# DoRA forward pass on one core: the first two stores issued two chunks earlier, and three small loads held back until the first store has landed

## The chip, the cores and the metric

One core of one Trainium2 chip. The metric is the device time of one execution in microseconds (us).

## The reference

```python
# x [16, 2048, 256], W [256, 256], lora_A [256, 16], lora_B [16, 256], m [256], scale = 1.0
W_adapted = W + scale * (lora_A @ lora_B)
W_norm = np.sqrt(np.sum(W_adapted ** 2, axis=0, keepdims=True) + 1e-8)
W_final = W_adapted / W_norm * m
y = x.reshape(-1, 256) @ W_final          # 32768 rows in, 32768 rows out
```

33.6 MB of x come in, 33.6 MB of y go out, and the weights are small.

## The kernel before

The 32768 rows are 8 blocks of 4096 rows, each of 8 chunks of 512 rows (64 chunks, 0-63). There is room on chip for five blocks. A block is loaded into a buffer, its chunks go through GpSimd (cast to bf16), TensorE (transpose and product), VectorE and ScalarE, and ScalarE copies each result chunk back over the x that it came from. The buffer is then stored and, once stored, loaded again with a later block. So blocks 5, 6 and 7 wait for the stores of blocks 0, 1 and 2.

All loads are issued by the sync engine on one queue, in order, all stores by the scalar engine on another. The number after a chunk range is the chunk behind whose copy the store is issued:

```python
loads = [(0, 2), (2, 2), (4, CH - 4)] + units[1 : XBUFS - 1]
loads += [((XBUFS - 1) * CH, CH - 3)]                          # block 4, chunks 32-36: 20 KB packets
loads += [(XBUFS * CH - 3 + c, 1) for c in range(3)] + units[XBUFS:]   # 37, 38, 39: 4 KB packets each
# ... (cut)
F = NBLK - XBUFS                                               # 3
G = F * CH                                                     # 24
stores = [(b * CH, CH, 21 + b) for b in range(F - 1)]          # blocks 0 and 1: 32 KB packets
stores += [(G - CH, CH // 2, 24), (G - CH // 2, CH // 2, 24)]  # block 2, two halves: 16 KB packets
FIRST = len(stores)
stores += [(G + c, 1, G + 3) for c in range(4)]                # chunks 24-27, 4 KB packets each
stores += [(G + 4, CH - 4, 47)]
stores += [(b * CH, CH, max(47, (b + 1) * CH - 1)) for b in range(F + 1, NBLK - 1)]
stores += [(g0, cnt, g0 + cnt - 1) for g0, cnt in units[-2:]]
HALF = FIRST - 2
# ... (cut)
for n in range(len(loads)):
    if loads[n][0] == XBUFS * CH:                              # block 5 waits for the first three stores
        for k in range(HALF + 1):
            nc.sync.wait_ge(sem(f"store{k}"), 16)
    if loads[n] == units[-1]:
        nc.sync.wait_ge(sem(f"store{HALF + 1}"), 16)
    load_x(n)
# ... (cut) GpSimd, one pair of chunks at a time:
    if p == REST:                                              # REST = 15
        nc.gpsimd.wait_ge(sem(f"store{HALF}"), 16)             # rests until the third store has landed
```

Each transfer is split over 16 DMA engines, 8 data packets per engine, one packet per partition. A packet of 32 KB takes 1.213 us, of 20 KB 0.766, of 16 KB 0.611, of 4 KB 0.159 (medians of this trace). These figures come from the trace's list of DMA packets, which gives the start, duration, size and queue of each but not its engine; I call them the packet records below. A time "per engine" is a sum over all packets divided by 16.

Of the kernel before, what the change touches and what calls it, by code (L numbers as in the profile page):

```python
# [11 lines left out]
def kernel(  # L12
# [10 lines left out]
    nc = tc.nc  # L23
# [19 lines left out]
    XBUFS = 5  # L43
    CH = DJ // J
# [59 lines left out]
    loads = [(0, 2), (2, 2), (4, CH - 4)] + units[1 : XBUFS - 1]  # L104
# [8 lines left out]

    F = NBLK - XBUFS
    G = F * CH
    stores = [(b * CH, CH, 21 + b) for b in range(F - 1)]
    stores += [(G - CH, CH // 2, 24), (G - CH // 2, CH // 2, 24)]
    FIRST = len(stores)
    stores += [(G + c, 1, G + 3) for c in range(4)]
# [9 lines left out]
    def sem(name):  # L129
        if name not in sems:  # L130
            sems[name] = tc.alloc_semaphore(name)
        return sems[name]
# [10 lines left out]
    def load_x(n):  # L143
        nc.sync.dma_start(
            out=in_sbuf(*loads[n]), in_=in_dram(x_flat, *loads[n])
        ).then_inc(sem(f"load{n}"), 16)
# [13 lines left out]
    nc.scalar.dma_start(out=b_nat[:], in_=lora_B).then_inc(sem("load_b"), 16)  # L160
    nc.scalar.dma_start(out=m_row[:], in_=m[None, :]).then_inc(sem("load_m"), 16)
    for n in range(len(loads)):
        if loads[n][0] == XBUFS * CH:


# [5 lines that stand above are left out]
# [13 lines left out]
    for p in range(NPR):  # L184
        b, c = divmod(p, PRB)
# [66 lines left out]
    for g in range(NCH):  # L252
        b, c = divmod(g, CH)
# [123 lines left out]
```

## Time and profile before

| | |
|---|---|
| median, 6 runs beside the changed kernel | 162.49 us (162.26 to 162.74) |
| span of the profiled run | 161.3 us |
| packet time, both queues, per engine | 158.4 us |
| empty DMA time before 4 us; from 158 us to the last packet's end at 160.8 (packet records) | 2.3 us; 1.0 us |
| last store issued | 132.2 us |

The page, its slices, the windows and the chain are shown in the prediction below. In short: the DMA engines are full from 3.2 us to the end, and no compute engine is. The first is from the table of waits, the others from GpSimd's timeline (start, duration, what, and in brackets the idle time before it and what ended it):

```profile
POOL xb L197 <- DMA out_dram<-x_sb: 27.7, 1, 27.7
```

```profile
93.86 5.57 POOL L197 CAST xb<-x_sb 128x2048 bf16<-128x2048 f32 x3 [3.25 <-DMA x_sb<-in_x_dram]
99.65 1.89 POOL L197 CAST xb<-x_sb 128x2048 bf16<-128x2048 f32 x1 [0.22 <-PE xt_ps L302]
```

GpSimd rests 27.7 us for the third store. Later it waits 3.25 us for the load of block 5.

### The profile page before, as it was taken

The page shows a single profiled execution, that of the slowest core. Times are in us where ns is not written, and L with a number is a line of the kernel's source. Part 1 is how long each engine was busy: PE and PEld are TensorE (multiplying, and loading weights), DVE is VectorE, ACT ScalarE, POOL GpSimd, SP SyncE. Part 2 cuts the span into 40 slices and gives each one's busy share as a digit, 9 for nine tenths or more (in the row PEclk, how much of TensorE's full clock was granted, in tenths as well). Part 3 has the DMA queues.
Part 4 walks back from the last instruction along what each step waited for, and adds up shares of the span by engine and source line. Part 5 has one row for each costly group of instructions (what it writes and reads, how often), then busy time and mean ns, then how long its engine had stood idle before and what let it go on. Part 6 is the DMA issues. An engine that isn't in the chain of part 4 may idle for free. (4 is left out here: it accounts for less than half of the span.)

```text
span 161.3 us, 2012 instructions
## 1 busy us (share of the span) xinstructions
PE 95.2 (59%) x786; PEld 83.8 (52%) x786; DVE 46.6 (29%) x44; ACT 63.9 (40%) x67; POOL 62.9 (39%) x39
## 2 busy tenths in 40 slices
PE   0491899999999700000199999999999940000000
PEld 0160799999998600000179989989899930000000
DVE  0439635353635300000033535353445300000000
ACT  3010076868686520000027675856776850000000
POOL 1085339776764000000674479198676200000000
PEclk9999999999999995555559999999999998555555
DMA  4999999999899999989999999999999999999995
GB/s 163 427 455 459 390 504 406 390 488 423 374 412 361 511 423 390 473 374 451 427 482 414 386 463 421 407 433 433 422 484 419 406 479 414 400 479 423 386 443 228
DMA packets 4356, 67.42 MB, mean 418 GB/s; under 512 B 625, under 2 KB 642, under 8 KB 1666
## 3 DMA queue, kind: packets, MB, share of 16 engines
q1 hardware_dynamic: 2160, 33.82, 49.5%
q10 hardware_dynamic: 2194, 33.59, 48.7%
q14 instruction: 2, 0.02, 0.0%
HBM read 33.85 MB, written 33.55 MB: 418 GB/s over the span
## 5 line engine op out<-in xcount | busy, mean ns | idle before, releaser
L256 ACT COPY x_sb<-y_ps 128x1024 f32<-128x1024 f32 x64 | 62.0, 1014 | 60.0 <-PE y_ps L316 57.8
L197 POOL CAST xb<-x_sb 128x2048 bf16<-128x2048 f32 x32 | 60.4, 1900 | 61.3 <-DMA out_dram<-x_sb 27.7
L316 PE MATMUL y_ps<-w_final,xt 128*128 128x256 bf16 x512 | 63.6, 278 | 1.2 <-PEq L291 1.1
L238 DVE COPY xt<-xt_ps 128x1024 f32<-128x1024 f32 x32 | 39.2, 1224 | 72.6 <-PE xt_ps L302 72.6
L316 PEld LDWEIGHTS y_ps<-w_final,xt 128*128 128x128 bf16 x512 | 51.1, 100 | 8.5 <-issue 1.9
L302 PE MATMUL xt_ps<-identity,xb 128*128 128x128 f32 x264 | 37.0, 287 | 28.2 <-PEq L291 28.2
L302 PEld LDWEIGHTS xt_ps<-identity,xb 128*128 128x128 f32 x264 | 31.7, 148 | 30.3 <-issue 30.0
L283 PE MATMUL y_ps<-sq,ones 128*128 128x256 f32 x4 | 2.1, 674 | 1.6 <-DVE sq L223 1.6
L272 PE MATMUL y_ps<-identity,a_nat 128*16 128x128 f32 x2 | 0.6, 394 | 4.1 <-DMA a_nat<-in_lora_A_dram 4.1
L248 ACT ACTIVATE norm<-y_ps,eps_col 128x256 f32<-128x256 f32 x1 | 0.5, 473 | 5.8 <-PE y_ps L283 5.8
L234 DVE TENSOR_TENSOR w_final<-wam,rnorm 128x256 bf16<-128x256 f32 x2 | 2.5, 1266 | 0.0
L283 PEld LDWEIGHTS y_ps<-sq,ones 128*128 128x128 f32 x4 | 1.2, 326 | 2.3 <-DVE sq L223 2.1
L272 PEld LDWEIGHTS y_ps<-identity,a_nat 128*16 128x16 f32 x2 | 0.1, 88 | 4.1 <-issue 4.1
L246 ACT ACT_TABLE_LOAD x1 | 1.3, 1283 | 2.4 <-issue 2.4
L203 POOL MEMSET xb<- 128x2048 bf16 x1 | 1.8, 1804 | 0.7 <-PE xt_ps L302 0.7
L231 DVE RECIPROCAL rnorm<-norm 128x256 f32<-128x256 f32 x1 | 1.7, 1747 | 0.0
L225 DVE COPY m_all<-y_ps 128x256 f32<-128x256 f32 x1 | 0.4, 424 | 3.3 <-PE y_ps L288 3.3
L214 DVE CAST b_bf<-b_nat 16x256 bf16<-16x256 f32 x1 | 0.3, 281 | 3.5 <-DMA b_nat<-in_lora_B_dram 3.5
L288 PE MATMUL y_ps<-m_row,ones 1*128 1x256 f32 x2 | 1.2, 706 | 0.0
L276 PE MATMUL y_ps<-b_bf,aT 16*128 16x256 bf16 x2 | 0.6, 404 | 0.7 <-DVE aT L216 0.7
L219 DVE SCALAR_TENSOR_TENSOR wa<-y_ps,w_nat 128x512 f32<-128x512 f32 x1 | 0.7, 692 | 0.8 <-PE y_ps L276 0.8
L288 PEld LDWEIGHTS y_ps<-m_row,ones 1*128 1x128 f32 x2 | 0.5, 308 | 0.6 <-issue 0.6
(13 smaller groups left out, 3.3 us busy)
## 6 DMA issues: line engine op xcount, KB each, us to landing
x_sb<-in_x_dram SPq DMA_DIRECT2D x5, 4096.0 KB, 26.5
out_dram<-x_sb ACTq DMA_DIRECT2D x5, 4096.0 KB, 22.7
out_dram<-x_sb ACTq DMA_DIRECT2D x5, 2048.0 KB, 29.0
x_sb<-in_x_dram SPq DMA_DIRECT2D x3, 2048.0 KB, 31.4
x_sb<-in_x_dram SPq DMA_DIRECT2D x1, 2560.0 KB, 44.8
x_sb<-in_x_dram SPq DMA_DIRECT2D x2, 1024.0 KB, 6.1
out_dram<-x_sb ACTq DMA_DIRECT2D x4, 512.0 KB, 50.1
x_sb<-in_x_dram SPq DMA_DIRECT2D x3, 512.0 KB, 46.4
```

The lines of the kernel that those rows point to most:

```text
L197: nc.gpsimd.tensor_copy(out=xb_bufs[p % NXB][:], in_=x_bufs[b % XBUFS][:, 2 * c * J : 2 * (c + 1) * J, :],).then_inc(sem("rounded"), 1)
L203: nc.gpsimd.memset(xb_bufs[NPR % NXB][:], 0.0).then_inc(sem("rounded"), 1)
L219: nc.vector.scalar_tensor_tensor(out=wa[:], in0=ab_ps, scalar=float(scale), in1=w_nat[:], op0=ALU.mult, op1=ALU.add).then_inc(dv, 1)
L231: nc.vector.reciprocal(out=rnorm[:], in_=norm[:]).then_inc(dv, 1)
L234: i = nc.vector.tensor_mul(out=w_final[:, t], in0=wam[:, t], in1=rnorm[:])
L238: nc.vector.tensor_copy(out=xt_bufs[p % NXT][:].rearrange("p r t -> p (r t)").bitcast(FP32), in_=xt_ps[p % 2][:],).then_inc(sem("copied"), 1)
L246: nc.scalar.activation(out=warm[:], in_=eps_col[:], func=AF.Sqrt)
L256: nc.scalar.copy(out=x_bufs[b % XBUFS][:, c * J : (c + 1) * J, :], in_=y_ps[g % 2][:]).then_inc(sem("room"), 1)
L283: i = nc.tensor.matmul(n2_ps, ones[:], sq[:, t, :], start=(t == 0), stop=(t == KC - 1))
L288: nc.tensor.matmul(mb_ps, ones[0:1, :], m_row[:], start=True, stop=True).then_inc(pe, 1)
L302: i = nc.tensor.transpose(xt_ps[p % 2][:, j * P : (j + 1) * P], xb_bufs[p % NXB][:, j, :].bitcast(FP32), identity[:],)
L316: i = nc.tensor.matmul(y_ps[h][:, j, :], xt_bufs[p % NXT][:, r : r + P, t], w_final[:, t, :], start=(t == 0 and (j % (J // 2)) == 0), stop ...
```

## The change

Intent: to have the first result on its way out earlier, and to keep the small loads out of its way until it has landed.

```diff
-    stores = [(b * CH, CH, 21 + b) for b in range(F - 1)]
+    stores = [(b * CH, CH, 19 + b) for b in range(F - 1)]
 ...
     for n in range(len(loads)):
+        if loads[n][0] == XBUFS * CH - 3:
+            nc.sync.wait_ge(sem("store0"), 16)
         if loads[n][0] == XBUFS * CH:
```

## The prediction

> **What bounds the kernel now.** I first read the head of the page and its slices, because a kernel that moves 67 MB in 161 us may be bound by moving it.
>
> ```profile
> span 161.3 us, 2012 instructions
> PE 95.2 (59%) x786; PEld 83.8 (52%) x786; DVE 46.6 (29%) x44; ACT 63.9 (40%) x67; POOL 62.9 (39%) x39
> PE   0491899999999700000199999999999940000000
> DMA  4999999999899999989999999999999999999995
> q1 hardware_dynamic: 2160, 33.82, 49.5%
> q10 hardware_dynamic: 2194, 33.59, 48.7%
> ```
>
> No compute engine passes 59%, PE has a hole of six slices in the middle and nothing to do in the last seven. The row of the DMA engines has no hole: below 9 only in the first, the last and two slices of 8 that border on a 9. The two queues (q1 the loads, issued by the sync engine; q10 the stores, issued by the scalar engine) take 49.5 + 48.7 = 98.2% of the 16 engines' time, 158.4 us each. Then where the missing 1.8% (2.9 us) lies, from a table of windows (the last columns are granted clock, DMA share, GB/s; a packet is booked where it starts, so a short window can exceed 1):
>
> ```profile
> 0.00:3.20 3.20, 0.00 (x0) 0.00 (x0) 0.17 (x2) 0.79 (x1) 0.70 (x6) 1.00 0.30 80
> 3.20:48.40 45.20, 37.84 (x294) 32.66 (x295) 22.06 (x23) 22.34 (x25) 26.74 (x15) 1.00 1.01 431
> 48.40:54.00 5.60, 5.50 (x52) 4.89 (x50) 2.55 (x3) 3.06 (x4) 1.77 (x1) 1.00 1.14 434
> 54.00:77.80 23.80, 1.62 (x14) 0.99 (x11) 0.97 (x1) 2.94 (x3) 0.00 (x0) 0.64 0.99 425
> 77.80:117.40 39.60, 36.64 (x309) 32.82 (x310) 15.87 (x13) 23.55 (x25) 27.38 (x15) 0.91 1.01 429
> 117.40:159.80 42.40, 13.63 (x125) 12.42 (x123) 4.94 (x5) 11.26 (x12) 6.33 (x4) 0.72 0.99 427
> ```
>
> All of it lies before 3.2 us (0.7 x 3.2 = 2.2 us) and after 159.8 us, where the engines end one after another. Between, DMA is full in every phase: loads alone, stores alone, loads beside stores. So the end is set by the sum of the transfers' times. Third, the chain of waits, to see what compute owes to the end:
>
> ```profile
> 130.19 1.01 ACT x_sb L256
> 131.21 0.92 ACTq L262
> ```
>
> It stops at 132.1 us, when the last store is issued; the 29 us after it are stores draining. Compute has that much slack at the end. Last, the scalar engine's order of work round the first stores, which the change moves:
>
> ```profile
> 43.88 1.93 ACT L256 COPY x_sb<-y_ps 128x1024 f32<-128x1024 f32 x2 [0.69 <-PE y_ps L316]
> 46.50 1.93 ACT L256 COPY x_sb<-y_ps 128x1024 f32<-128x1024 f32 x2 [0.69 <-PE y_ps L316]
> 48.53 0.37 ACTq L149 DMA_DIRECT2D out_dram<-x_sb  x1
> 49.12 1.01 ACT L256 COPY x_sb<-y_ps 128x1024 f32<-128x1024 f32 x1 [0.69 <-PE y_ps L316]
> 50.24 0.37 ACTq L149 DMA_DIRECT2D out_dram<-x_sb  x1
> ```
>
> Pairs of chunks are copied every 2.62 us; the copy at 46.50 is of chunks 20 and 21, and the first store follows it at 48.53, the second after chunk 22 at 50.24.
>
> **What the Trainium skill says.** "DMA: Bandwidth & Descriptors", section "Where 436 GB/s comes from", puts the ceiling at 435 GB/s, for the ports of all 16 engines together; "HBM Reference", section "Specifications (TRN2)", says a core alone is bound by its 16 DMA engines, at about 425. The trace agrees: 425 to 434 in the windows above, whichever queues run. So there is no faster mix to be had, only gaps to close or open. "DMA: Bandwidth & Descriptors", section "Queues, rings and completion order", says each engine goes round-robin between queue rows by packet. The packet records agree in steady state: from 82 to 110 us one 32 KB load packet (1.213 us) and one 4 KB store packet (0.159 us) alternate nearly everywhere. They disagree just after a newcomer is issued: the store issued at 48.53 has its first packet at 52.63 (4.1 us), after nearly all of the 4 KB loads, and the load issued at 77.92 has its first at 81.63 (3.7 us). Section "Latency and other measured facts" gives about 0.6 us to the first byte; with idle engines at the start of this trace, most engines' first packet came at 2.55 us for issues at 0.9, so 1.6 us.
>
> **The change, part by part.**
> Removed and added instructions: none but one wait on the sync queue. Bytes and packet shapes are the same, so the 158.4 us of packets stay, but for the following.
>
> (1) First store after chunk 19 instead of 21: the copies at 43.88 end at 45.81, so it is issued at about 45.9, 2.6 us earlier; the second after chunk 20 at about 47.6. The scalar engine's copy of chunk 21 slips by about 0.5 us, as the one after the second store does now; compute then waits from 58 us anyway (27.7 us of GpSimd waiting for a store in the table of waits), so this costs nothing.
>
> (2) Holding the three 4 KB loads. Today the 20 KB packets of block 4 end at 48.3 to 48.55 and the 4 KB ones fill the engines until 52.7, covering the latency of the first store. Held back, nothing is queued behind the 20 KB packets but the first store. If it needs the 4.1 us seen today, it comes at 50.0 and all engines idle 50.0 - 48.4 = 1.6 us. If it needs the idle figure of 1.6 us it is there at 47.5 and there is no gap; if it needs that and the 1.2 us to read one 32 KB packet, it comes at 48.7 and the gap is 0.3. Since the 3.7 and 4.1 us could be a fixed delay or about 100 KB of work already taken in by each engine (6 packets of 16 KB, or 26 of 4 KB), and in the second case only what is left of the 20 KB packets stands ahead, I choose a gap of 0.6 us, an estimate.
>
> (3) What the move saves. The three 4 KB loads took 1.29, 1.41 and 1.69 us per engine (128 packets each; the mean packet was 162, 176 and 211 ns) against 8 x 0.159 = 1.27 each, as the late 4 KB stores have it in the mix. So 4.39 - 3.81 = 0.58 us was lost as the first store cut in. After the change they run one to one beside large store packets; I count 0.5 us saved.
>
> (4) Order afterwards. First store 48.9 to about 58.7, landing near 59; the held loads are issued then and join near 62.5. From there one 4 KB load packet goes with each store packet. The third store (which frees block 0's buffers and GpSimd) lands after three stores and about 12 load packets per engine: 49.0 + 9.7 + 9.7 + 4.9 + 12 x 0.16 + 0.5 = 75.7, against 77.8 now, 2 us earlier. GpSimd's long wait gets shorter by that. Yet the next large load sits in one queue behind the rest of the 4 KB loads (24 per engine in all), so its first packet stays near 82, as now. The last 4 KB load lands near 82.5, and compute wants it five pairs after the release, at about 86: no new wait.
>
> Sum: 162.4 + 0.6 - 0.5 = 162.5; I say 162.4, since the two terms are of one size and only the gap is uncertain.
>
> **The rivals.**
> A gap replaces the overlap: the first store comes only 4 us after its issue into empty engines, and its stream has one queue. Speaks for it: 3.7 and 4.1 us, seen twice. Against: the start of the trace, at 1.6. It gives 162.4 + 1.6 - 0.5 = 163.5.
> The earlier release of GpSimd is worth its 2 us: the long idle of PE (58 to 80 us) tempts one to this, 160.4. Against: DMA is full in that idle time, and nothing in the last 29 us waits for compute. Bytes still have to move.
> The held loads arrive late and stall compute, chunk 47's store is issued later and a hole opens near 115 us, when loads and small stores run out. Today that store is issued at 110.85 and its first packet is at 115.83, so the margin is 1 to 2 us. In (4) the loads come with 3 us to spare; if the joining delay were far worse, 1 to 2 us would be lost: 164.
> Pure reordering, with no gap and no saving: 162.4.
>
> **Range and chances.** Faster by 2% needs 159.1 us, less than the start's 2.2 us plus the packets' 158.4, so only faster packets could do it: 2%. Slower by 2% needs 165.6, 3.2 us of empty engines; even the full 1.6 us gap with the hole near 115 hardly gets there: 4%. Within 2%: 94%. Range: from no gap, with the saving and a slightly more even finish (161.6), to the full gap (163.5).
>
> **What would show it.** Right: queue shares again near 98%; the windows full after the first stores; the first store issued near 45.9; the third landing near 75 to 76; the GpSimd wait about 2 us shorter with no gain at the end. A window of 48.4 to 50 with a DMA share well under 1 confirms the gap and sizes step 2. 4 KB loads with a mean packet near 160 ns confirm step 3. Wrong: DMA slices below 9 later on, above all near 115 us; GpSimd waiting for a load near 86 us; large packets that take more than 1.22 us.

## The result

| | median | runs |
|---|---|---|
| before | 162.49 us | 6 (162.26 to 162.74) |
| changed | 162.61 us | 6 (162.50 to 163.24) |

The ratio is 1.0012, with a 95% interval of 0.9993 to 1.0031: the same. Ratios here are the mean time of one kernel's fast runs over the mean of the other's fast runs of the same rounds, so not quite the ratio of the quoted medians. Those of the experiments below come out of the recorded times only when each kernel's first run, for the variants the profiled one, is left out; the medians have it in.

The head of the changed kernel's page, and its queues:

```profile
span 161.3 us, 2012 instructions
PE 98.1 (61%) x786; PEld 85.6 (53%) x786; DVE 46.6 (29%) x44; ACT 64.1 (40%) x67; POOL 62.9 (39%) x39
PE   0490899999997920000799949999999980000000
DMA  5999999999899999899999999999999999999994
q1 hardware_dynamic: 2160, 33.82, 49.2%
q10 hardware_dynamic: 2194, 33.59, 48.9%
```

The DMA row again has no hole, and the queues' shares add up to 98.1% instead of 98.2%. The hole in PE's row is one slice shorter and compute's work has moved, but not the end. The same windows as before:

```profile
0.00:3.20 3.20, 0.00 (x0) 0.00 (x0) 0.17 (x2) 0.79 (x1) 0.70 (x6) 1.00 0.36 86
3.20:48.40 45.20, 38.04 (x286) 32.45 (x287) 21.95 (x22) 21.55 (x24) 26.48 (x14) 1.00 1.02 436
48.40:54.00 5.60, 4.78 (x45) 4.21 (x44) 2.45 (x2) 3.34 (x4) 1.92 (x2) 1.00 0.96 415
54.00:77.80 23.80, 3.24 (x29) 2.56 (x27) 1.23 (x1) 3.55 (x4) 2.06 (x2) 0.61 1.00 429
77.80:117.40 39.60, 37.00 (x296) 32.70 (x297) 14.70 (x12) 22.91 (x24) 24.22 (x13) 0.89 1.00 424
117.40:159.80 42.40, 15.08 (x139) 13.72 (x136) 6.12 (x5) 11.97 (x13) 7.49 (x4) 0.70 0.99 427
```

The window from 48.4 us, where I feared a gap, has a share of 0.96 with the bookings at packet starts; in the packet records the last 20 KB load packets end from 48.28 to 48.50 us, the first 32 KB store packets start at 48.28, and the packet times between 44 and 56 us fill all 16 engines, so there is no gap. The scalar engine round the first stores:

```profile
44.76 1.93 ACT L258 COPY x_sb<-y_ps 128x1024 f32<-128x1024 f32 x2 [0.69 <-PE y_ps L318]
46.79 0.37 ACTq L149 DMA_DIRECT2D out_dram<-x_sb  x1
47.38 1.01 ACT L258 COPY x_sb<-y_ps 128x1024 f32<-128x1024 f32 x1 [0.69 <-PE y_ps L318]
48.50 1.08 ACTq L149 DMA_DIRECT2D out_dram<-x_sb  x1
```

The first store is issued at 46.79 us, 1.7 us earlier than before (in this run compute was 0.9 us behind; in e5, e8 and e9 below, which have the same code up to there, it was issued at 45.3 to 45.4 us). The waits and the chain:

```profile
POOL xb L199 <- DMA out_dram<-x_sb: 24.7, 1, 24.7
```

```profile
131.65 1.01 ACT x_sb L258
132.66 0.91 ACTq L264
```

GpSimd's rest is 3.0 us shorter and ends at 75.7 instead of 77.9 us. Yet the chain ends at 133.6 us instead of 132.1: compute was released earlier and finished later. That I had not foreseen. GpSimd's timeline shows where, to be read against the two lines above:

```profile
94.03 5.57 POOL L199 CAST xb<-x_sb 128x2048 bf16<-128x2048 f32 x3 [5.21 <-DMA x_sb<-in_x_dram]
101.49 1.89 POOL L199 CAST xb<-x_sb 128x2048 bf16<-128x2048 f32 x1 [1.89 <-PE xt_ps L304]
```

Block 5 arrives when it did, because its load is set by the DMA and not by compute. So the earlier release became a longer wait (5.21 instead of 3.25 us), after which GpSimd now stands behind TensorE for 1.89 us. Windows of the changed kernel, then of the kernel before (the columns after the length are the busy time and count of PE, PEld, DVE, ACT and POOL, then granted clock, DMA share, GB/s):

```profile
94.00:98.00 4.00, 1.92 (x13) 1.68 (x14) 0.78 (x1) 0.85 (x1) 3.96 (x3) 0.87 1.03 442
98.00:102.00 4.00, 4.00 (x28) 3.25 (x26) 0.98 (x2) 2.02 (x2) 2.11 (x2) 0.70 0.99 426
```

```profile
94.00:98.00 4.00, 3.64 (x34) 3.14 (x32) 2.05 (x2) 2.07 (x4) 4.00 (x3) 1.00 0.96 413
98.00:102.00 4.00, 4.00 (x39) 3.77 (x37) 1.45 (x2) 3.31 (x4) 3.33 (x2) 1.00 1.00 431
```

TensorE's timeline shows its idle time in brackets, again changed kernel first:

```profile
96.08 1.11 PE L304 MATMUL xt_ps<-identity,xb 128*128 128x128 f32 x8 [2.32 <-PEq L293]
```

```profile
95.90 1.06 PE L302 MATMUL xt_ps<-identity,xb 128*128 128x128 f32 x8 [0.36 <-PEq L291]
```

TensorE stood idle for 2.32 us (0.36 us before), and its granted clock (the share of full speed that it is allowed) fell to a half from 96.96 to 100.37 us. 28 matmuls fitted into the second window instead of 39. The stores behind chunk 47 are issued at 112.23 instead of 110.85 us. The DMA engines did not notice: their share is 1.03 and 0.99 meanwhile. It is not an accident of one trace. A fall of the clock between 95 and 102 us stands also in e4, e8, e9 and e11 below, where GpSimd's rest ended at 75.8 to 76.6 us, and in none of e1, e2, e6, e7, e10 and the kernel before, where it ended at 77.6 to 78.6. (e3, whose block 5 came only at 98.8 us, has such a fall too; e5, without the rest, has others.)

### The profile page after: what moved, and what is told of

Its sections match the earlier page's. It is cut to its first block, busy times and chain, and to the rows that moved or that the text cites. A ratio compares the mean times of both kernels' runs of the same rounds, so it can differ in the third digit from the quotient of the medians.

```text
span 161.3 us, 2012 instructions
## 1 busy us (share of the span) xinstructions
PE 98.1 (61%) x786; PEld 85.6 (53%) x786; DVE 46.6 (29%) x44; ACT 64.1 (40%) x67; POOL 62.9 (39%) x39
## 5 line engine op out<-in xcount | busy, mean ns | idle before, releaser
L318 PE MATMUL y_ps<-w_final,xt 128*128 128x256 bf16 x512 | 66.5, 286 | 2.5 <-PEq L293 2.5
L318 PEld LDWEIGHTS y_ps<-w_final,xt 128*128 128x128 bf16 x512 | 52.3, 103 | 10.9 <-issue 3.2
L304 PEld LDWEIGHTS xt_ps<-identity,xb 128*128 128x128 f32 x264 | 32.3, 150 | 27.7 <-issue 27.2
```

Of the source, the lines that this page charges most:

```text
L304: i = nc.tensor.transpose(xt_ps[p % 2][:, j * P : (j + 1) * P], xb_bufs[p % NXB][:, j, :].bitcast(FP32), identity[:],)
L318: i = nc.tensor.matmul(y_ps[h][:, j, :], xt_bufs[p % NXT][:, r : r + P, t], w_final[:, t, :], start=(t == 0 and (j % (J // 2)) == 0), stop ...
```

## The experiments

Two theories were held against each other. The first: the end is the start-up, plus the sum of all packet times, plus any empty time of the DMA engines; order and compute matter only where they open a hole or stretch packets. Its rivals: a fixed delay of about 4 us for a new transfer, an end that compute still helps to set, or two real effects of the change that cancel.

"Before" in each line means the kernel before on the same chip in the same rounds. "Stretch" is the sum of what packets took beyond the median of their size, per engine, from the packet records.

### e1: the early stores alone

```diff
-        if loads[n][0] == XBUFS * CH - 3:
-            nc.sync.wait_ge(sem("store0"), 16)
```

> The stores behind chunks 19 and 20, the 4 KB loads not held. Theory 'sum of packets': no gap anywhere, so 162.2 to 162.7, within 0.3% of before. The first store packet follows the backlog: if an engine drains about 100 KB that it has already taken in, it comes near 50.5 (issue near 46 to 47, plus 3.7 to 4.1 us). The 4 KB loads again lose some 0.3 to 0.6 us (mean packet over 170 ns) when the store cuts in. Rival 'holding is what costs or saves': this would differ from the full change by over 0.5 us.

Measured: 162.94 us against 162.47, ratio 1.0022 (1.0004 to 1.0041). The first store was issued at 45.67 us and had its first packet at 49.84, 4.17 us later and after a number of 4 KB loads, as expected. The first 4 KB load took 216 ns per packet instead of 159 (0.45 us of stretch) and the 20 KB load 817 ns instead of 766 (0.41 us; this one I had not expected). The median lies a little above the range that I gave. The stretched packets are not the reason: the profiled run's span is 0.78 us longer than that of the kernel before, its packet time only 0.07 us (158.43 against 158.36), since the weights' load lost less at the start; the rest is empty time before 4 us (2.5 against 2.3) and at the end (1.4 against 1.0). The full change differs from e1 by 0.3 us of medians, from other rounds: with the stores early, holding the loads is worth next to nothing either way. And as the early stores gain nothing by themselves, there is no gain that the cost of the hold could cancel.

### e2: the hold alone

```diff
-    stores = [(b * CH, CH, 19 + b) for b in range(F - 1)]
+    stores = [(b * CH, CH, 21 + b) for b in range(F - 1)]
```

> Only the hold: the first store still behind chunk 21, issued near 48.5 to 49.4, when the loads have run out at 48.5. Theory 'backlog' (a new transfer waits only for what the engines took in): first store packet about 1.5 us after its issue, an empty stretch of 1.5 to 2.5 us, and the time longer by that less up to 0.5: 163.4 to 164.5. Rival 'fixed joining delay of 3.7 to 4.1 us': empty for 3.7 to 5 us, 165.5 to 167.

Measured: 164.97 us against 162.47, ratio 1.0142 (1.0092 to 1.0191). The issue, from the scalar engine's timeline, and the windows around it:

```profile
49.37 0.37 ACTq L149 DMA_DIRECT2D out_dram<-x_sb  x1
```

```profile
46.00:48.40 2.40, 2.40 (x24) 2.21 (x23) 1.22 (x1) 1.71 (x3) 1.89 (x1) 1.00 0.96 410
48.40:50.20 1.80, 1.80 (x19) 1.65 (x18) 1.12 (x1) 1.11 (x2) 1.09 (x1) 1.00 0.00 0
50.20:54.00 3.80, 3.69 (x35) 3.24 (x33) 1.33 (x2) 2.79 (x3) 0.80 (x1) 1.00 1.17 500
```

From 48.58 to 50.24 us nothing moves at all (packet records), while every compute engine works. The first store packet comes at 50.24 us, 0.87 us after the issue. So a fixed delay of 4 us is ruled out, and so is my expectation of 1.5 us. The time grew by 2.5 us of medians: in the profiled run 1.82 us of emptiness (the mean of the 16 engines) and 0.52 us more packet time (158.88 against 158.36). The latter is a balance: about 0.5 us were lost in the second 32 KB store (mean packet 1281 ns) when the small loads joined it, 0.4 in a 16 KB store and 0.3 in a 16 KB load, and 0.8 us less than before in the 4 KB loads and the weights' load. The time is above the range that I gave by 0.5 us, for that second reason. The four runs lie wide apart (163.99 to 165.66), so it is the trace, not the time, that tells the two theories apart.

### e3: the hold, with the stores one pair later still

```diff
-    stores = [(b * CH, CH, 19 + b) for b in range(F - 1)]
+    stores = [(b * CH, CH, 23 + b) for b in range(F - 1)]
```

> The hold, and the first stores behind chunks 23 and 24: issued one pair (2.62 us) later than in the run with the hold alone. If empty DMA time goes into the end one for one, the empty stretch and the time grow by 2.6 us against that run: 166 to 167.2. Rival 'compute has slack that takes it up': no growth.

Measured: 167.81 us against 162.47, ratio 1.0327 (1.0294 to 1.036).

```profile
51.91 0.37 ACTq L149 DMA_DIRECT2D out_dram<-x_sb  x1
```

```profile
48.40:52.80 4.40, 4.40 (x43) 4.07 (x41) 2.41 (x2) 3.01 (x4) 1.89 (x1) 1.00 0.09 37
```

Issued 2.54 us later than in e2, first packet again 0.87 us after the issue (52.78), empty time 4.38 us instead of 1.82 (2.56 more), and 2.84 us more of time; that is 0.6 us over the range, with e2 already 0.5 us over its own. Empty DMA time goes into the end about one for one, though the last store is issued 26 us before the end even here (140.1 us).

### e4: 2.1 MB not stored (wrong)

```diff
-    stores += [(b * CH, CH, max(47, (b + 1) * CH - 1)) for b in range(F + 1, NBLK - 1)]
+    stores += [(b * CH, CH // 2 if b == F + 1 else CH, max(47, (b + 1) * CH - 1)) for b in range(F + 1, NBLK - 1)]
```

> Wrong on purpose: of the changed kernel, the second half of block 4's result (2.1 MB) is not stored; compute is whole. If the end is the sum of packets, a half of a 32 KB store of 9.7 us goes: 4.85 us shorter, 157.6 to 158.0. Rival 'compute or a wait sets part of the end': less than 3 us.

Measured: 158.12 us against 162.47, ratio 0.9724 (0.9701 to 0.9746), and 4.5 us under the changed kernel. Of the 4.85 us, the packet time lost 4.83 (153.51 against 158.34); 0.5 us of empty time at the start and the end, 3.8 against 3.3 us in the two profiled runs, stand against it. Its chain and its windows:

```profile
138.17 1.01 ACT x_sb L258
139.18 0.92 ACTq L264
```

```profile
3.20:155.00 151.80, 99.96 (x786) 87.17 (x786) 46.45 (x42) 63.44 (x67) 62.33 (x33) 0.86 1.00 428
```

In this run compute finished 6.5 us later than in the changed kernel's, and the end still came earlier by the bytes taken out. Compute does not set the end.

### e5: GpSimd doesn't rest

```diff
-        if p == REST:
-            nc.gpsimd.wait_ge(sem(f"store{HALF}"), 16)
```

> The changed kernel with GpSimd's wait for the third store taken out, so compute runs on to the chunks whose loads are held (it stops for the first 4 KB load near 72 instead). If compute is off the path: 162.3 to 163. Rival 'an earlier release of compute is worth time': over 1 us shorter.

Measured: 163.41 us against 162.51, ratio 1.0062 (1.0044 to 1.008). The profiled run of the four was the fastest, 162.74. This is 0.4 us above my range. An earlier release of compute gains nothing; it seems to cost 0.6%. Nor does compute end earlier by it: GpSimd waits for block 5 until 94.08 us (94.03 in the changed kernel), and the stores behind chunk 47 are issued at 112.08 (112.23 there). Why the time grew is not in the trace that I have: its packet time is the smallest of all the full kernels (158.07 us), its DMA row has no hole, and the end is as uneven as elsewhere. That stays open.

### e6 and e7: the three 4 KB loads as one load of 12 KB packets

```diff
-    loads += [(XBUFS * CH - 3 + c, 1) for c in range(3)] + units[XBUFS:]
+    loads += [(XBUFS * CH - 3, 3)] + units[XBUFS:]
```

e6 has this edit in the kernel before, e7 in the changed kernel.

> The kernel before with the three 4 KB loads as one load with 12 KB packets. If the 0.57 us by which the 4 KB loads exceed their nominal time comes from being small while a 32 KB store cuts in, most of it goes, and larger packets save about 0.1: 0.3 to 0.7 us shorter than before. Rival 'the loss goes with the cutting in, whatever the packet': no change.

> The changed kernel with the held loads as one load with 12 KB packets (8 per engine). They pass in the second and third store; loads of block 5 then join beside 16 KB stores or 4 KB stores. If 0.31 us are lost by the 16 KB stores because small packets follow, part of it goes: 0 to 0.5 us shorter than the changed kernel. The rival: block 5's loads come earlier against the small stores, and the loss moves to these: no change.

Measured: e6 162.69 us against 162.51, ratio 1.0012 (0.9998 to 1.0026). A miss: the 12 KB packets took 586 ns in the mean when the store cut in, against 462 in e7, where they ran in company, which is 8 x 0.124 = 1.0 us of stretch and more than the 4 KB packets had. Packets get stretched when a newcomer cuts in, whatever their size; the rival was right. e7: 163.03 us against 162.51, ratio 1.004 (1.0017 to 1.0064), so no gain either; that it is 0.4 us above the changed kernel (other rounds) is not explained, as its packet time is 0.25 us less. The stretch had moved: 0.22 us in the 20 KB load and 0.29 in the 16 KB loads near 116 us, next to none in the 16 KB stores.

### e8, e9 and e10: how near the hole at 116 us is

The stores due behind chunk 47 put off, to chunk 49 in the changed kernel (e8), to chunk 51 in the changed kernel (e9) and in the kernel before (e10):

```diff
-    stores += [(G + 4, CH - 4, 47)]
-    stores += [(b * CH, CH, max(47, (b + 1) * CH - 1)) for b in range(F + 1, NBLK - 1)]
+    stores += [(G + 4, CH - 4, 51)]
+    stores += [(b * CH, CH, max(51, (b + 1) * CH - 1)) for b in range(F + 1, NBLK - 1)]
```

> The changed kernel, the stores due behind chunk 47 put off to chunk 49 (2.6 us). In the changed kernel their first packet came 0.57 us before the loads ran out, so a put-off of 2.6 us should open a hole of about 2 us near 116 and cost that: 164 to 165. If the joining delay shrinks to 1.5 us when nothing is queued, the issue at 114.85 gives a first packet at 116.4 and the cost is only 0.2 to 0.5 us.

> The changed kernel with the stores due behind chunk 47 put off to chunk 51: issued near 117.5. The loads ran out at 116.2 to 116.4, so with a first packet 0.9 us after the issue (as the runs with the hold alone showed on empty engines) a hole of 2.0 us opens near 117 and costs as much: 164.2 to 165. Rival 'compute's finish and the stores' issue have slack to the end': no change from the changed kernel.

> The same put-off in the kernel before: issue near 110.85 + 5.24 = 116.1, first packet near 117.0, loads and small stores run out at 117.4: no hole, or at most 0.3 us, so 162.3 to 162.9. If it costs as much as in the changed kernel, the margin near 116 did not shrink by the change.

| | issue | first packet | empty near 116 | median | ratio to before |
|---|---|---|---|---|---|
| e8 | 114.84 | 115.71 | 0 | 162.71 us | 1.0039 (1.0008 to 1.007) |
| e9 | 117.84 | 118.69 | 2.8 us | 165.12 us | 1.0152 (1.0101 to 1.0203) |
| e10 | 115.94 | 116.78 | 0.6 us | 163.25 us | 1.0053 (1.0013 to 1.0092) |

The columns are from the packet records and the timeline; the empty time is the mean of the 16 engines. The hole of e9 in its windows:

```profile
112.00:116.20 4.20, 4.20 (x41) 3.85 (x40) 2.45 (x2) 2.81 (x4) 3.06 (x2) 1.00 0.87 372
116.20:118.20 2.00, 2.00 (x21) 1.89 (x19) 0.65 (x1) 1.53 (x2) 1.34 (x2) 1.00 0.00 0
```

e8 kept clear of it and came out below both costs that I had named (0.1 us above the changed kernel, from other rounds), because a new store joins 0.87 us after its issue when little stands ahead. e9 fell in, for 2.5 us of time (165.12 against 162.61 of the changed kernel, from other rounds), 0.1 us over my range. e10, whose loads and small stores ran out at 116.55 us and not at the 117.4 that I had taken over, lost 0.7 us, over twice what I had allowed. For the same put-off, the changed kernel's store is issued 1.9 us later than the old one's. So in these traces the change did use up margin near 116 us, unseen in its own time.

### e11: the first stores much earlier

```diff
-    stores = [(b * CH, CH, 19 + b) for b in range(F - 1)]
+    stores = [(b * CH, CH, 15 + b) for b in range(F - 1)]
```

> The changed kernel, its first stores behind chunks 15 and 16, some 10 us earlier than behind 19 and 20: they join near 40 among the 32 KB loads. By the sum of packets earlier is worth nothing: 162.3 to 163.2, the spread being what newcomers cost in stretched packets (0.3 to 0.6 us in the other runs). Rival 'earlier stores bring the end forward': 2 us or more shorter.

Measured: 163.07 us against 162.59, ratio 1.0035 (1.0017 to 1.0053). Issued at 40.11 us, first packet at 44.35 (4.24 us later). The 20 KB load took 861 ns per packet instead of 766, 0.8 us of stretch, nearly all of it from 42 to 44 us, just before the store's first packet. An issue 5 to 7 us earlier than in the changed kernel's runs gains nothing.

### What a new transfer waits for

All first stores together (us; packet records and timeline):

| run | issue | first packet | between | ahead of it |
|---|---|---|---|---|
| e11 | 40.11 | 44.35 | 4.24 | 32 and 20 KB loads, more behind |
| e1 | 45.67 | 49.84 | 4.17 | 20 and 4 KB loads |
| e6 | 47.95 | 52.25 | 4.30 | 20 and 12 KB loads |
| e10 | 48.21 | 52.46 | 4.25 | 20 and 4 KB loads |
| before | 48.53 | 52.63 | 4.10 | 4 KB loads |
| e9 | 45.29 | 48.36 | 3.07 | rest of the 20 KB load |
| e5 | 45.31 | 48.21 | 2.90 | rest of the 20 KB load |
| e7 | 45.36 | 48.26 | 2.90 | rest of the 20 KB load |
| e8 | 45.36 | 48.39 | 3.03 | rest of the 20 KB load |
| e4 | 46.43 | 48.26 | 1.83 | rest of the 20 KB load |
| changed | 46.79 | 48.28 | 1.49 | rest of the 20 KB load |
| e2 | 49.37 | 50.24 | 0.87 | nothing |
| e3 | 51.91 | 52.78 | 0.87 | nothing |

Issued up to 1.5 us apart, the stores of e9 and of the changed kernel start within 0.1 us of each other: when the load ahead is done. So the wait is what the engines still have to do, up to about 4.2 us of it, and 0.87 us if there is nothing. The held loads tell the same from the other queue: in the changed kernel they are issued at 58.89 us and have their first packet at 62.98, 4.09 us later. That the 4.2 us are work already taken in is the reading that fits all the rows; no run looks inside an engine. Whether the limit counts bytes (about 110 KB per engine, an estimate from 1.213 us for 32 KB) or time, no run separates. The stretched packets lie in this same wait, between the newcomer's issue and its first packet: from 50 us in the kernel before (wait from 48.53 to 52.63), from 47 in e1 (45.67 to 49.84), from 42 in e11 (40.11 to 44.35). "Cutting in" therefore begins before the newcomer's own packets show; why is not in the records.

## Why the prediction was right, and where it was not

Predicted 162.4 us, range 161.6 to 163.5; measured 162.61. By its steps:

- **The bound.** The sum of the packets sets the end: right, shown by e4 (packets out, time out) and by e2, e3 and e9 (empty time in, time in). But the 29 us of slack that I read off the chain belong to the last store alone. The stores behind chunk 47 had far less: putting them off by some 5 us left the DMA engines empty for 0.6 us in the kernel before (e10) and for 2.8 us in the changed one (e9), which cost that one 2.5 us.
- **Step 1.** Right in kind. The 2.6 us became 1.7 in the profiled run, as compute was behind in it, and cost nothing.
- **Step 2, the gap.** Put at 0.6 us, measured 0. The fixed delay that made me keep 1.6 us in the range is ruled out; of the two readings that I named, the work already taken in is the one that fits all the runs. The idle figure of 1.6 us was also read too late: in that trace the first packets of the weights' load start at 1.96 us for an issue at 0.94, and e2 and e3 gave 0.87. I should have trusted that reading: the move of the stores is just what keeps the hold harmless. Without it, e2 pays 2.5 us.
- **Step 3, the saving.** Put at 0.5 us, measured near 0. The 4 KB loads did come out at 159 ns per packet (0.57 us of stretch gone). But 0.34 us came back in a 16 KB store (mean 654 ns instead of 611) when block 5's loads cut in, and the rest in several places, 0.12 of it in the weights' load at the start. The total stretch was 1.13 us before and 1.11 after, packet time 158.36 and 158.34. The cost belongs to the cutting in, not to the small packets (e6), and the change moves it.
- Steps 2 and 3 were each wrong by 0.5 to 0.6 us in opposite directions, so the sum was closer than its terms; that was luck. Some of it is the run's: in e5, e8 and e9, whose first store was issued 1.4 to 1.5 us earlier than in the changed kernel's profiled run, the 20 KB load lost 0.3 us that this run did not lose.
- **Step 4.** The third store landed at 75.7 (75.7 predicted), the large load's first packet came at 82.29 (near 82), the last 4 KB load landed at 83.06 (82.5), in time for a cast that began at 86.93. GpSimd's wait shrank by 3.0 us (2), for no gain. Not foreseen: the earlier release turned into a longer wait, a half clock for 3.41 us and a store issued 1.4 us later.
- **The rivals.** The worth of an earlier release is refuted by the result itself (3.0 us earlier, no gain) and by e5. The hole near 115 us did not open, but it is real (e9), and nearer than before (e10).

What stays open: e1, e5, e7, e8, e10 and e11 are 0.2 to 0.6% slower than the kernel before, by intervals that leave out 1. Only e10 has a hole for it, of 0.6 us, and in its profiled run a more even end (0.5 us empty instead of 1.0) makes up for most of that. The packet sums don't explain the others, and the empty time at the start (2.1 to 2.5 us in these traces) and at the end (0.5 to 1.5) differs by as much from trace to trace. The account above holds for effects of 1 us and more.

None of the ten variants with a whole result is faster than the kernel before, and packets plus start-up leave little room.

## What to carry to other kernels

When the DMA engines are full from start to end, the order of transfers is worth nothing by itself; look for what can empty them, and for how long. If you hold a load back, make sure another transfer is issued before the queue's last work is done: here a store issued 1.5 us ahead hid itself entirely, and one issued 0.9 us too late cost 2.5 us. And check what an earlier release of an idle engine leads to: it may only move its wait to a place where it delays the work further, as the half clock did here.

## What the Trainium skill lacked or had wrong

- "DMA: Bandwidth & Descriptors", section "Queues, rings and completion order": its round-robin by packet holds in steady state, but it doesn't tell of the joining delay. Here the first store, on the second queue, waited 4.10 to 4.30 us from its issue while the first queue had enough in it, 1.49 to 3.07 when that ran out sooner, and 0.87 when it was empty.
- The same page, section "Latency and other measured facts", gives about 0.6 us to the first byte. Here it was 0.87 us from the start of the issue, of which the issue itself took 0.37; 0.5 us after its end.
- No page that I read has the cost of a newcomer: packets of the running transfer are stretched, by 0.3 to 1.0 us in all (12 KB packets 586 ns instead of 462, 4 KB ones up to 216 instead of 159, 16 KB ones 654 instead of 611).
- "TensorE: Matmul & The Clock Gate", section "Part 1: The HAM clock gate", puts the fall to half clock after an idle window of about 3.4 us. Here the clock was halved for 3.41 us after only 2.32 us without a matmul: in the 3.41 us before the fall (93.55 to 96.96) TensorE was busy for 1.09 us. In e4, e8, e9 and e11 it was busy for 0.7 to 1.25 us of the 3.41 before such a fall; in e2, with 1.82 us without a matmul and 1.65 us busy from 96.52 to 99.93, there was none.
